# A two-layer decoder trunk on one core: TensorE's order written out for the whole mixer, query weights in the gated blocks' ring, norm factors of the queries in the exponentials' scale

## The chip, the cores and the metric

The kernel runs on one core of a Trainium2 chip. The core has TensorE (PE, matmuls, with weight loads shown apart as PEld), VectorE (DVE), ScalarE (ACT), GpSimd (POOL) and SyncE (SP, which issues most transfers). The metric is the device time of one execution in microseconds (us), lower is better.

## The reference

Two layers on 512 tokens of width 1024, all float32. Each layer is a half-step feed-forward, a mixer, a second half-step feed-forward and a norm. The mixer, which the change touches:

```python
n = rms_norm(h, mix_norm[l])
u_conv, q, k, v, q_mem = jnp.split(n @ w_in[l], splits, axis=-1)   # 768, 384, 128, 128, 256 columns
y_conv = conv_module(u_conv, ...)       # a * sigmoid(gate), causal depthwise conv of 31 taps, layer norm, silu
q = apply_rope(rms_norm(q per head of 64, swa_q_norm[l]), cos, sin)     # 6 heads; k the same, 2 heads
y_swa = sliding_window_attention(q, k, v, swa_sinks[l])                 # blocks of 128, window 128, a sink per head
qm = rms_norm(q_mem per head, mem_q_norm[l])                            # 4 heads
y_mem = memory_attention(qm, mk, mv)                                    # 256 memory tokens
h = h + jnp.concatenate([y_conv, y_swa, y_mem], axis=-1) @ w_out[l]
```

## The kernel before

Activations lie transposed, channels on partitions and 512 tokens along the row. Each float32 product is three products of split operands (`mm3`: hi*hi, lo*hi, hi*lo). A weight tile is loaded to a `raw` tile (3 buffers, SP's queue) and split into `whi` (a rounded copy, ScalarE) and `wlo` (the rest), four buffers each. `wlo` is made in one of two ways: with `V`, VectorE subtracts (L142); with `G`, ScalarE writes -x into it (L147) and GpSimd issues a second transfer of the same weights that adds x (L148). "The gated blocks' ring" is the pool of four `ghi`/`glo` pairs in which the feed-forward keeps its gated activations; the mixer keeps its outputs `y` there.

The engines' instruction streams are put in order by a planner when the program is built: program order is priority, an instruction goes where the planner's own times find room, and a block under `queued()` must follow, on its engine, the last TensorE instruction noted before it (`tail`). On the chip each engine runs its stream in that fixed order.

The mixer's steps follow ORDER (L45). `c0`, `c1`: each conv channel group is two halves (the value and the gate), 24 matmuls each over all tokens; `gate` multiplies by R, the row norm, and by the sigmoid. With c0's first half the sums for the norm are made (rc, a column per token), with its second half R. `q`: for each of four token blocks t, 24 matmuls give 128 tokens by 512 columns (six query heads, two key heads); ScalarE copies them to a half-buffer of the ring `q` (L676) and squares them (L530), VectorE sums the squares (L532, L533), GpSimd raises to the power -1/2 (L189) and makes the rotated part in a second half-buffer of the ring (L682), VectorE multiplies, adds (L686, L688), scales each head by its factor (L537), TensorE transposes the four 128-column pieces (L561) and ScalarE writes qT and kT. `v`: the same for values and memory queries. `a`: attention in ten groups of score blocks (`scored`: scores and minimum, since the columns carry a minus sign; `turned`: exponentials, transposes; `weighted`, `scaled`, `attended`); c20 and c21, the two halves of group c2, are issued inside it. `t0` to `t2`: the taps, 31 passes of VectorE per group (L850, L853), the lowest priority. `s`: layer norm and silu. Then the output product: for eight output blocks first the five attention pieces, then the three conv pieces. PSUM banks: three `mm` and one `cf` taken in turn by `mm()`, two `po`, two `pt`.

Of the kernel before, what the change touches and what calls it, by code (L numbers as in the profile page):

```python
# [10 lines left out]
F32 = mybir.dt.float32  # L11
# [33 lines left out]
ORDER = "c0 c1 q v a t0 t1 t2 s"  # L45
# [14 lines left out]
def trunk(ctx: ExitStack, tc: tile.TileContext, xT, memT, pos, w1a, w3a, w2a, w1b, w3b, w2b,  # L60
# [96 lines left out]
    def weights(src, cols, on):  # L157
        hi, lo = pair()
# [361 lines left out]
    A.activation(maskr, cst[:, 0 : P + 256], AF.Copy)  # L520
# [6 lines left out]
    def head_scale(ps, col, n):  # L527
# [6 lines left out]
        return rsq(v, n)  # L534
# [22 lines left out]
    def to_columns(dst, src, n, tag="pt"):  # L557

        pt = bank([P, n, P], tag)
        for c in range(n):  # L560
            T.transpose(pt[:, c, :], src[:, blk(c)], ident)  # L561
        if dst is not None:
            A.activation(dst, pt[:, 0 : dst.shape[1], :], AF.Copy)
        return pt

    def memory(l):
# [20 lines left out]
        for t in range(2):  # L587
# [6 lines left out]
            A.activation(mT[:, :, blk(t)], to_columns(None, q, 2, "mm"), AF.Copy, scale=-(HD**-0.5))  # L594
# [7 lines left out]
    def mixer(l, x, st, last):  # L602
# [14 lines left out]
        gg = [tmp.tile([P, 2, S], F32, tag="g", name="gg", bufs=2) for _ in range(2)]  # L617
        rings = {"pr": [uu[:, 0], uu[:, 1], tm("pr", "pr", 1)], "q": [x[:, i] for x in gg for i in range(2)],
                 "ptb": [scratch[0][:, blk(i, S)] for i in range(2)], "yn": [scratch[1][:, blk(i, CCH)] for i in range(2)],
                 "cv": [scratch[2][:, blk(i, S)] for i in range(2)]}  # L620
# [39 lines left out]
        conv_halves = []  # L660

        def conv_in(c):
            for i in range(2):
                conv_half(c, i)
            for i in range(2):
                gate(c, i)


        def queries():
            ww = [weights(wqk[l, i], 1024, G) for i in range(4)]  # L670
            for t in range(NT):
                ps = mm()
                for k in range(KD):
                    mm3(ps, at(x, ALL, k, blk(t)), at(ww[k // 2], ALL, blk(k % 2, 512)), k == 0, k == KD - 1)
                q = ring("q")
                A.activation(q, ps, AF.Copy, scale=rc[:, t : t + 1])  # L676
                r = head_scale(ps, rc[:, t : t + 1], 8)
                q2 = ring("q")
                qv, q2v = (z.rearrange("p (h s e) -> p h s e", s=2, e=32) for z in (q, q2))
                for i, (h0, n) in enumerate(((0, NH), (NH, 2))):  # L680
                    for half in range(2):
                        G.tensor_tensor(out=q2v[:, h0 : h0 + n, half, :], in0=qv[:, h0 : h0 + n, 1 - half, :],  # L682
                                        in1=sg[:, t, i, half].unsqueeze(1).to_broadcast([P, n, 32]), op=ALU.mult)
                for i, (h0, n) in enumerate(((0, NH), (NH, 2))):
                    z = heads(q)[:, h0 : h0 + n, :]
                    V.tensor_tensor(out=z, in0=z, in1=cg[:, t, i].rearrange("p s e -> p (s e)").unsqueeze(1).to_broadcast([P, n, HD]),  # L686
# [332 lines left out]
```

## Time and profile before

| | |
|---|---|
| time, median of 3 runs | 1838.69 us (1835.46 to 1841.57) |
| the profiled execution: its time, its span | 1838.87 us, 1836.9 us |
| mean granted TensorE clock | 0.984 |
| busy, share of the span: PE, PEld, DVE, ACT, POOL | 97%, 86%, 71%, 48%, 9% |
| DMA | 243.62 MB, mean 133 GB/s |
| chain that ended last | PE 79%, DVE 11%, issue 7% |

A busy share is a mean over the whole span; the mixers are some 380 to 573 us and 1280 to 1480 us of it. "Idle before" is the time in which an engine stood before an instruction, with what ended the wait.

### The profile page before, as it was taken

The page shows a single profiled execution, that of the slowest core. Times are in us where ns is not written, and L with a number is a line of the kernel's source. Part 1 is how long each engine was busy: PE and PEld are TensorE (multiplying, and loading weights), DVE is VectorE, ACT ScalarE, POOL GpSimd, SP SyncE. Part 2 cuts the span into 40 slices and gives each one's busy share as a digit, 9 for nine tenths or more (in the row PEclk, how much of TensorE's full clock was granted, in tenths as well). Part 3 has the DMA queues.
Part 4 walks back from the last instruction along what each step waited for, and adds up shares of the span by engine and source line. Part 5 has one row for each costly group of instructions (what it writes and reads, how often), then busy time and mean ns, then how long its engine had stood idle before and what let it go on. Part 6 is the DMA issues. An engine that isn't in the chain of part 4 may idle for free.

```text
span 1836.9 us, 28081 instructions
## 1 busy us (share of the span) xinstructions
PE 1773.1 (97%) x10996; PEld 1585.7 (86%) x10996; DVE 1301.3 (71%) x1918; ACT 880.6 (48%) x1350; POOL 173.7 (9%) x179
## 2 busy tenths in 40 slices
PE   8999999997999999999999999999979999999997
PEld 6889999876778989898888898988867879898986
DVE  8967666679757867575678685756788577675755
ACT  4546444444546535353655453535346455353532
POOL 2002000005001000000010010000240010000000
PEclk9999999998999999999999999999979999999998
DMA  7456655262038456565555474643420575474722
GB/s 243 110 166 174 171 135 150 58 155 68 16 91 203 109 145 169 142 165 140 156 132 150 142 185 137 167 115 109 97 71 10 145 161 151 134 181 123 173 77 80
DMA packets 91284, 243.62 MB, mean 133 GB/s; under 512 B 9360, under 2 KB 11664, under 8 KB 91152
## 3 DMA queue, kind: packets, MB, share of 16 engines
q1 hardware_dynamic: 77040, 190.45, 33.9%
q0 software_dynamic: 14112, 51.39, 15.6%
q8 instruction: 86, 1.41, 0.3%
q14 instruction: 46, 0.38, 0.1%
HBM read 239.70 MB, written 2.10 MB: 132 GB/s over the span
## 4 chain that ended last, share of the span: by engine, by line
PE 79%; DVE 11%; issue 7%; ACT 1%; DMA 1%; POOL 0%; SPq 0%; DVEq 0%; POOLq 0%; ACTq 0%
PE mm L173 11%; PE mm L172 11%; PE mm L174 11%; PE po L172 9%; PE po L173 9%; PE po L174 9%; PE pt L173 6%; PE pt L172 6%; PE pt L174 6%; DVE there L853 4%; DVE wlo L142 1%; DVE xlo L152 1%; DVE st L240 1%; DVE nmw L745 1%; PE cf L172 1%
## 5 line engine op out<-in xcount | busy, mean ns | idle before, releaser
L141 ACT ACTIVATE whi<-raw 128x1024 fp32r<-128x1024 f32 (+4 forms) x384 | 353.6, 924 | 510.1 <-PE mm L173 240.8
L142 DVE TENSOR_TENSOR wlo<-raw,whi 128x1024 fp32r<-128x1024 f32 (+4 forms) x384 | 404.7, 1056 | 134.7 <-ACT whi L141 133.2
L173 PE MATMUL mm<-glo,whi 128*128 128x512 f32 x752 | 293.8, 391 | 0.0
L174 PE MATMUL mm<-ghi,wlo 128*128 128x512 f32 x752 | 292.9, 389 | 0.0
L172 PE MATMUL mm<-ghi,whi 128*128 128x512 f32 x752 | 291.0, 390 | 0.0
L174 PE MATMUL po<-mh,wlo 128*128 128x256 f32 x864 | 244.6, 283 | 1.4 <-DVE wlo L142 1.4
L172 PE MATMUL pt<-xhi,whi 128*128 128x256 f32 x864 | 243.2, 283 | 2.1 <-ACT xhi L141 2.0
L173 PE MATMUL pt<-xlo,whi 128*128 128x256 f32 x864 | 243.8, 283 | 1.6 <-DVE xlo L142 1.6
L172 PE MATMUL po<-mh,whi 128*128 128x256 f32 x864 | 244.8, 283 | 0.4 <-ACT part L380 0.4
L173 PE MATMUL po<-ml,whi 128*128 128x256 f32 x864 | 244.6, 283 | 0.0
L174 PE MATMUL pt<-xhi,wlo 128*128 128x256 f32 x864 | 243.7, 283 | 0.0
L458 DVE SCALAR_TENSOR_TENSOR h<-mm,h 128x512 f32<-128x512 f32 x128 | 87.7, 688 | 138.5 <-PE mm L174 138.4
L172 PEld LDWEIGHTS pt<-xhi,whi 128*128 128x128 f32 x864 | 165.1, 192 | 3.6 <-ACT xhi L141 2.4
L173 PEld LDWEIGHTS pt<-xlo,whi 128*128 128x128 f32 x864 | 165.7, 192 | 2.6 <-DVE xlo L142 1.8
L174 PEld LDWEIGHTS po<-mh,wlo 128*128 128x128 f32 x864 | 165.8, 192 | 1.6 <-DVE wlo L142 1.6
L172 PEld LDWEIGHTS po<-mh,whi 128*128 128x128 f32 x864 | 165.8, 192 | 1.5 <-ACT part L380 0.8
L174 PEld LDWEIGHTS mm<-ghi,wlo 128*128 128x128 f32 x752 | 141.2, 188 | 29.7 <-issue 0.5
L172 PEld LDWEIGHTS mm<-ghi,whi 128*128 128x128 f32 x752 | 141.1, 188 | 29.3 <-DVE h L458 1.2
L173 PEld LDWEIGHTS po<-ml,whi 128*128 128x128 f32 x864 | 165.8, 192 | 0.6
L173 PEld LDWEIGHTS mm<-glo,whi 128*128 128x128 f32 x752 | 141.3, 188 | 28.3 <-issue 0.5
L174 PEld LDWEIGHTS pt<-xhi,wlo 128*128 128x128 f32 x864 | 165.5, 192 | 0.0
L853 DVE SCALAR_TENSOR_TENSOR there<-ypad,par,there 128x512 f32<-128x512 f32 x180 | 133.4, 755 | 1.0
(283 smaller groups left out, 3243.4 us busy)
## 6 DMA issues: line engine op xcount, KB each, us to landing
raw<-in_w2a SPq DMA_DIRECT2D x48, 384.0 KB, 3.7
raw<-in_w2b SPq DMA_DIRECT2D x48, 384.0 KB, 3.6
raw<-in_w1b SPq DMA_DIRECT2D x26, 512.0 KB, 3.7
raw<-in_w3b SPq DMA_DIRECT2D x26, 512.0 KB, 3.7
raw<-in_w1a SPq DMA_DIRECT2D x25, 512.0 KB, 3.7
raw<-in_w3a SPq DMA_DIRECT2D x25, 512.0 KB, 4.2
wsum<-in_w1a SPq DMA_DIRECT2D x18, 512.0 KB, 4.5
wsum<-in_w3a SPq DMA_DIRECT2D x18, 512.0 KB, 4.5
```

The source lines that it names most:

```text
L141: A.activation(hi, x, AF.Copy)
L142: on.tensor_tensor(out=lo, in0=x, in1=hi.bitcast(F32), op=ALU.subtract)
L152: V.scalar_tensor_tensor(out=lo, in0=x, scalar=col, in1=hi.bitcast(F32), op0=ALU.mult, op1=ALU.subtract)
L172: T.matmul(ps, a[0], b[0], start=first, stop=False, **more)
L173: T.matmul(ps, a[0], b[1], start=False, stop=False, **more)
L174: tail[0] = T.matmul(ps, a[1], b[0], start=False, stop=last, **more)
L240: V.tensor_tensor(out=self.sums[0], in0=self.sums[0], in1=sq, op=ALU.add)
L458: V.scalar_tensor_tensor(out=h[:, d, :], in0=ps, scalar=0.5, in1=h[:, d, :], op0=ALU.mult, op1=ALU.add)
L745: V.tensor_reduce(out=each(nmw, i), in_=pp[i], axis=AX.X, op=ALU.min)
L853: V.scalar_tensor_tensor(out=cv[:, c, :], in0=ypad[:, c, j : j + S], scalar=conv_w[:, c, j : j + 1], in1=cv[:, c, :], op0=ALU.mult, op1=AL ...
```

## The change

`ORDER` names every conv half, query block, value block and transposition on its own, and all of them are put under `queued()`, so TensorE's order is that of the list. The transpositions (`Q0` to `Q3`, `V0` to `V3`) are steps of their own, each some steps behind its block. c20 stands in the list; c21 follows the first scores. The query weights, and those of c20 and c21, take pairs of the gated ring (`spare()`); the four pairs for `y` are taken later, inside attention and in reverse. Every query block has its own buffer, with q2 in the two halves of `uu`. The query heads and the memory queries are transposed without their norm factors (rq, rm): scores take a maximum, one small VectorE step multiplies it by minus the factor, and the exponential gets the factor as its scale; only the two key heads are scaled before the transposition. The minus sign leaves kT and mT and goes into the mask. c1, c2 and the first four output products' weights are split with `G`; the sums for the sinks (esw) go from VectorE to GpSimd.

```diff
-ORDER = "c0 c1 q v a t0 t1 t2 s"
+ORDER = "c00 c01 q0 c10 q1 Q0 c11 q2 Q1 v0 q3 Q2 v1 v2 Q3 V0 v3 V1 c20 V2 V3 a t0 t1 t2 s"
...
-    def weights(src, cols, on):
-        hi, lo = pair()
+    def weights(src, cols, on, own=None):
+        hi, lo = own or pair()
...
-    A.activation(maskr, cst[:, 0 : P + 256], AF.Copy)
+    A.activation(maskr[:, 0:P], cst[:, 0:P], AF.Copy)
+    A.activation(maskr[:, P : P + 256], cst[:, P : P + 256], AF.Copy, scale=-1.0)
...
-    def head_scale(ps, col, n):
+    def head_scale(ps, col, n, out=None):
...
-        return rsq(v, n)
+        if out is None:
+            return rsq(v, n)
+        G.tensor_tensor(out=out, in0=v, in1=nhalf[:, 0:n], op=ALU.pow)
...
-        gg = [tmp.tile([P, 2, S], F32, tag="g", name="gg", bufs=2) for _ in range(2)]
-        rings = {"pr": [uu[:, 0], uu[:, 1], tm("pr", "pr", 1)], "q": [x[:, i] for x in gg for i in range(2)],
...
+        query = [tmp.tile([P, 2, S], F32, tag="g", name="query", bufs=2) for _ in range(2)]
...
+        def spare():
+
+            return tuple(z.rearrange("p i s -> p (i s)") for z in gated_pair())
...
-            with queued() if c == 2 or 2 * c + i < 3 else nullcontext():
-                project(ps, weights(wconv[l, c, i], 1024, V), x)
+            with queued():
+                project(ps, weights(wconv[l, c, i], 1024, G if c else V, spare() if c == 2 else None), x)
...
-            conv_halves.append(ps)
-            if c == 2:
-                gate(c, i)
+            halves.append((c, i, ps))
+            while halves and R is not None:
+                gate(*halves.pop(0))
...
+        def queries(t):
+            if not t:
+                ww["q"] = [weights(wqk[l, i], 1024, G, spare()) for i in range(4)]
+            ps = mm()
+            with queued():
                 for k in range(KD):
...
+            q, q2 = query[t // 2][:, t % 2], uu[:, t % 2]
+            A.activation(q, ps, AF.Copy, scale=rc[:, t : t + 1])
+            head_scale(ps, rc[:, t : t + 1], 8, rq[:, t, :])
...
+            V.tensor_tensor(out=q, in0=q, in1=q2, op=ALU.add)
+            per_head(q[:, CCH:], rq[:, t, NH:], 2)
+
+        def query_columns(t):
+            with queued():
+                pt = to_columns(qT[:, :, blk(t)], query[t // 2][:, t % 2], 4)
+            A.activation(kT[:, blk(t)], pt[:, CC, :], AF.Copy, scale=HD**-0.5)
...
+        def values(t):
+            if not t:
+                ww["v"] = [weights(wvm[l, i], 768, V) for i in range(4)]
...
-                per_head(q, head_scale(ps[:, 0:256], rc[:, t : t + 1], NM), NM)
-                to_columns(qmT[:, :, blk(t)], q, 2, "po")
+            q = scratch[0][:, blk(t, 256)]
+            A.activation(q, ps[:, 0:256], AF.Copy, scale=rc[:, t : t + 1])
+            head_scale(ps[:, 0:256], rc[:, t : t + 1], NM, rm[:, t, :])
+
+        def value_columns(t):
+            with queued():
+                to_columns(qmT[:, :, blk(t)], scratch[0][:, blk(t, 256)], 2, "po")
...
-                    V.tensor_reduce(out=nmr[:, b, i], in_=pp[i], axis=AX.X, op=ALU.min)
+                    V.tensor_reduce(out=nmr[:, b, i], in_=pp[i], axis=AX.X, op=ALU.max)
+                V.scalar_tensor_tensor(out=nmr[:, b], in0=nmr[:, b], scalar=-1.0, in1=by_half(rm[:, b, :]), op0=ALU.mult, op1=ALU.mult)
...
-                V.tensor_reduce(out=each(nmw, i), in_=pp[i], axis=AX.X, op=ALU.min)
+                V.tensor_reduce(out=each(nmw, i), in_=pp[i], axis=AX.X, op=ALU.max)
+            V.scalar_tensor_tensor(out=at_(nmw), in0=at_(nmw), scalar=-1.0, in1=rr, op0=ALU.mult, op1=ALU.mult)
...
-            V.tensor_tensor(out=at_(esw), in0=at_(nmw), in1=per(sinks), op=ALU.add)
+            G.tensor_tensor(out=at_(esw), in0=at_(nmw), in1=per(sinks), op=ALU.add)
...
-                A.activation(pr[:, i, 0:W], scores[i], AF.Exp, bias=nm[:, b, i, c : c + 1], scale=-1.0)
+                n = 2 * c + i
+                A.activation(pr[:, i, 0:W], scores[i], AF.Exp, bias=nm[:, b, i, c : c + 1], scale=rr[:, b, n : n + 1])
...
             s = scored(GROUPS[0][0], GROUPS[0][1:])
+            conv_half(2, 1)
+            yy.extend([gated_pair() for _ in range(KD // 2)][::-1])
+            y.extend(at(p, ALL, i, ALL) for p in yy for i in range(2))
...
-                if n < 2:
-                    conv_half(2, n)
                 nxt_s = None
-                if 2 <= n + 1 < len(GROUPS):
+                if n + 1 < len(GROUPS):
...
-            w = weights(wout[l, d, :, CCH:], 640, V)
+            w = weights(wout[l, d, :, CCH:], 640, G if d < 4 else V)
```

## Rows read from the trace of the kernel before

**Rows 1.** The page's first part: busy time of each engine, its share of the span, and the count of its instructions.

```profile
PE 1773.1 (97%) x10996; PEld 1585.7 (86%) x10996; DVE 1301.3 (71%) x1918; ACT 880.6 (48%) x1350; POOL 173.7 (9%) x179
```

**Rows 2.** Busy time by stage, the two mixer stretches (us): length, busy time of PE, PEld, DVE, ACT and POOL with the count of instructions, mean granted clock of PE, DMA share, GB/s.

```profile
380.00:573.00 193.00, 174.76 (x937) 143.51 (x936) 148.77 (x273) 95.60 (x180) 39.21 (x37) 0.95 0.34 87
1280.00:1480.00 200.00, 181.61 (x959) 148.43 (x957) 152.59 (x273) 99.28 (x186) 39.00 (x37) 0.94 0.35 91
```

**Rows 3.** The same view in narrower slices, around the second half of the queries and values in layer 0 and layer 1.

```profile
440.00:460.00 20.00, 6.54 (x28) 3.92 (x26) 20.00 (x42) 8.61 (x21) 7.28 (x5) 0.65 0.21 66
448.00:464.00 16.00, 8.43 (x27) 5.54 (x28) 15.86 (x32) 6.16 (x14) 4.81 (x4) 0.50 0.13 41
1346.00:1366.00 20.00, 7.63 (x35) 5.04 (x34) 20.00 (x39) 10.36 (x23) 7.29 (x5) 0.61 0.21 67
```

**Rows 4.** TensorE's waits, first in 376 to 575 us, then in 1281 to 1473 us: what waited for whom, us in total, times, longest.

```profile
PE pt L561 <- DVE gg L537: 8.1, 1, 8.1
PE po L561 <- DVE gg L537: 4.6, 2, 3.0
PE mm L173 <- DVE xlo L152: 1.4, 4, 0.6
PE po L561 <- DVE hv L533: 0.9, 1, 0.9
...
PE pt L561 <- DVE gg L537: 6.3, 1, 6.3
```

**Rows 5.** TensorE's timeline: start, us, line, operation. First eight score matmuls in the hole and eight later; then, in layer 1, two transposes of L561 with the wait ahead of them (in brackets), the first matmul of c20 and what follows its last, and the same of c21.

```profile
454.77 2.08 PE L730 MATMUL mm<-mT,there 64*128 64x256 f32 x8 [0.47 <-ACT there L563]
487.30 1.14 PE L730 MATMUL mm<-here 64*128 64x256 f32 x8
1358.79 0.66 PE L561 MATMUL po<-cst,gg 128*128 128x128 f32 x2 [3.03 <-DVE gg L537]
1365.83 0.66 PE L561 MATMUL po<-cst,gg 128*128 128x128 f32 x2 [1.60 <-DVE gg L537]
1366.14 0.78 PE L172 MATMUL po<-xhi,whi 128*128 128x512 f32 x1
1373.98 1.03 PE L761 MATMUL pt<-cst,uu 128*128 128x128 f32 x8
1377.36 0.50 PE L172 MATMUL po<-xhi,whi 128*128 128x512 f32 x1
1382.93 0.51 PE L724 MATMUL mm<-maskr 128*128 128x384 f32 x2
```

**Rows 6.** Timelines of ScalarE, VectorE and GpSimd in layer 0: the fourth query block from its copy to its scaling.

```profile
434.82 0.70 ACT L676 ACTIVATE gg<-cf,rc 128x512 f32<-128x512 f32 x1
442.02 0.16 DVE L533 TENSOR_SCALAR hv<-hs 128x8 f32<-128x8 f32 x1
442.33 2.48 POOL L189 TENSOR_TENSOR rsq<-hv,nhalf 128x8 f32<-128x8 f32 x1 [3.16 <-DVE hv L533]
448.69 0.68 DVE L537 TENSOR_TENSOR gg<-gg,rsq 128x512 f32<-128x512 f32 x1
```

**Rows 7.** The query weights: SP's raw loads in layer 0, GpSimd's issue of the last accumulating transfer, and, for all accumulating transfers of L148, the time from issue to landing.

```profile
374.72 10.18 SPq L99 DMA_DIRECT2D raw<-in_wqk  x4
403.20 0.86 POOL L148 DMA_DIRECT2D wlo<-in_wqk  x1 [4.62 <-ACT wlo L147]
DMA to landing us min/median/max: 5.6/7.8/10.4
```

**Rows 8.** GpSimd's power -1/2, groups by line and shape: count, busy us and mean ns of one, idle before.

```profile
L189 POOL TENSOR_TENSOR rsq<-hv,nhalf 128x8 f32<-128x8 f32 x8 | 19.7, 2458 | 18.5 <-DVE hv L533 18.5
L189 POOL TENSOR_TENSOR rsq<-hv,nhalf 128x4 f32<-128x4 f32 x12 | 19.6, 1636 | 77.2 <-DVE hv L533 77.2
L189 POOL TENSOR_TENSOR rsq<-ms,nhalf 128x4 f32<-128x4 f32 x9 | 9.6, 1068 | 154.9 <-DVE ms L203 153.7 <-DVE pf L481 1.2
```

**Rows 9.** VectorE's share of the work: busy times from the first gate to the output product in layer 0 and layer 1; the taps (L853), ns min/median/max; and groups by shape of layer 0 in 391.5 to 519.9 us.

```profile
391.50:519.20 127.70, 110.84 (x642) 91.74 (x641) 114.20 (x216) 60.49 (x129) 31.68 (x29) 0.92 0.21 52
1297.00:1424.00 127.00, 111.72 (x648) 92.68 (x647) 112.67 (x210) 61.85 (x129) 31.64 (x29) 0.92 0.20 52
L853 DVE SCALAR_TENSOR_TENSOR there<-ypad,par,there x180: 720/742/1086, 394.9 to 1421.4; 128x512 f32<-128x512 f32 x180
...
L142 DVE TENSOR_TENSOR wlo<-raw,whi 128x640 fp32r<-128x640 f32 x4 | 3.3, 814 | 0.0
L537 DVE TENSOR_TENSOR gg<-gg,rsq 128x512 f32<-128x512 f32 x4 | 3.1, 777 | 0.2 <-POOL rsq L189 0.2
L142 DVE TENSOR_TENSOR wlo<-raw,whi 128x1024 fp32r<-128x1024 f32 x2 | 2.4, 1214 | 0.0
L537 DVE TENSOR_TENSOR gg<-gg,rsq 128x256 f32<-128x256 f32 x4 | 1.6, 411 | 0.0
```

**Rows 10.** Timelines of VectorE and TensorE at the mixer's end in layer 0: the last tap, the start of the output product, the low part of the last conv output, the first matmul that takes conv outputs.

```profile
516.53 0.75 DVE L853 SCALAR_TENSOR_TENSOR there<-ypad,par,there 128x512 f32<-128x512 f32 x1
518.92 0.95 PE L172 MATMUL mm<-ghi,whi 128*128 128x512 f32 x3
546.35 0.69 DVE L142 TENSOR_TENSOR glo<-aux,ghi 128x512 fp32r<-128x512 f32 x1 [1.08 <-ACT ghi L141]
549.90 0.39 PE L172 MATMUL mm<-ghi,whi 128*128 128x512 f32 x1
```

More of the change, by code (lines that the diff above doesn't have):

```diff
@@ L560, in to_columns @@
         for c in range(n):
-            T.transpose(pt[:, c, :], src[:, blk(c)], ident)
+            tail[0] = T.transpose(pt[:, c, :], src[:, blk(c)], ident)
         if dst is not None:
@@ L626, in ring @@
             return r[-1]
-        yy = [gated_pair() for _ in range(KD // 2)]
-        y = [at(p, ALL, i, ALL) for p in yy for i in range(2)]
         R, rc = None, const.tile([P, NT], F32, tag="rc", name="rc")
+        ww = {}
+        def spare():
+            return tuple(z.rearrange("p i s -> p (i s)") for z in gated_pair())
         def conv_half(c, i):
@@ L644, in conv_half, with gate @@
                         R = kept(spread(rc), "R")
-            conv_halves.append(ps)
-            if c == 2:
-                gate(c, i)
-        def gate(c, i):
+            halves.append((c, i, ps))
+            while halves and R is not None:
+                gate(*halves.pop(0))
+        halves = []
+        def gate(c, i, ps):
             u = ypad[:, c, PAD:]
-            ps = conv_halves.pop(0)
             if not i:
@@ L658, in gate @@
             V.tensor_tensor(out=u, in0=u, in1=s, op=ALU.mult)
[L660 to L672, printed above, removed]
-                for k in range(KD):
[L674 to L686, printed above, removed]
-                                    op=ALU.mult)
-                V.tensor_tensor(out=q, in0=q, in1=q2, op=ALU.add)
-                per_head(q, r, 8)
-                pt = to_columns(qT[:, :, blk(t)], q, 4)
-                A.activation(kT[:, blk(t)], pt[:, CC, :], AF.Copy, scale=-(HD**-0.5))
@@ L694, in values @@
-        def values():
-            ww = [weights(wvm[l, i], 768, V) for i in range(4)]
-            for t in range(NT):
-                ps = mm()
-                for k in range(KD):
-                    mm3(ps[:, 0:CCH], at(x, ALL, k, blk(t)), at(ww[k // 2], ALL, blk(k % 2, CCH)), k == 0, k == KD - 1)
-                A.activation(vn[:, t, :, 0:HD], heads(ps[:, 256:CCH]), AF.Copy, scale=rc[:, t : t + 1])
-                q = ring("q")[:, 0:256]
-                A.activation(q, ps[:, 0:256], AF.Copy, scale=rc[:, t : t + 1])
-                per_head(q, head_scale(ps[:, 0:256], rc[:, t : t + 1], NM), NM)
-                to_columns(qmT[:, :, blk(t)], q, 2, "po")
+        rq = const.tile([P, NT, 8], F32, tag="rq", name="rq")
@@ L710, in mixer @@
+        def value_columns(t):
+            with queued():
+                to_columns(qmT[:, :, blk(t)], scratch[0][:, blk(t, 256)], 2, "po")
+        yy, y = [], []
         nmw, esw = (const.tile([P, NT, 2, CC], F32, tag=t, name=t) for t in ("nmw", "esw"))
         nmr = const.tile([P, NT, 2, 2], F32, tag="nmr", name="nmr")
-        sinks, nsinks = (z.rearrange("p (c i) -> p i c", i=2) for z in (sink, nsink[:, l, :]))
+        by_half = lambda z: z.rearrange("p (c i) -> p i c", i=2)
+        sinks, nsinks = by_half(sink), by_half(nsink[:, l, :])
@@ L875, in mixer @@
         for step in ORDER.split():
-            f = {"c": conv_in, "q": queries, "v": values, "a": attention, "t": taps, "s": swish}[step[0]]
+            f = {"c": conv_half, "q": queries, "Q": query_columns, "v": values, "V": value_columns, "a": attention, "t": taps,
+                 "s": swish}[step[0]]
             f(*map(int, step[1:]))
```

26 lines of the change are left out of this document (20 added, 6 removed).

## The prediction

> **What bounds the kernel now.** I read the totals first: TensorE is busy for 97% of the span [rows 1], so at most some 60 us of plain idleness can be won anywhere, and every other engine has room on average. The second view is the busy time by stage: the two mixer stretches hold 174.8 us of TensorE in 193 us and 181.6 us in 200 us, at a mean granted clock of 0.95 and 0.94 [rows 2]. About 18 us is lost in each of two stretches that make a fifth of the span. Cutting them into 20 us slices shows one hole: in 440 to 460 us TensorE works 6.5 us of 20 while VectorE works all 20, and the granted clock is 0.65 there, with 0.50, the lower of its two levels (1.2 GHz for 2.4), all through 448 to 464 us; layer 1 has the same hole at 1346 us [rows 3]. The third view, TensorE's own waits, names it: the transposes of L561, queries and memory queries, wait 8.1 + 4.6 + 0.9 us in layer 0 [rows 4] and 6.3 + 3.0 + 1.6 us in layer 1 [rows 4, 5] for VectorE's L537 and L533, the norm factors.
>
> The timelines show why the factors are late. ScalarE takes the fourth query block out of PSUM only at 434.8 us, behind the columns of an earlier one, because the ring "q" has four half-buffers and each block takes two (q and q2). After that its chain is long: its mean square is ready at 442.0, GpSimd's power starts at 442.3 and takes 2.5 us, and VectorE's L537 starts at 448.7, 13.9 us after the copy [rows 6]. TensorE has nothing else in that time: c20 (L638, group c2) stands behind attention's first scores, and these behind the transposes. The clock halves in the hole, which costs again after it: eight score matmuls take 2.08 us against 1.14 us later, and c20 in layer 1 takes 1373.98 - 1366.14 = 7.84 us where c21 takes 1382.93 - 1377.36 = 5.57 us [rows 5].
>
> **What the change wins.** TensorE's instructions are the same in number and size; what can go is the waiting and the half clock.
> 1. Layer 0's waits on L561, and the L730 that follows: 8.1 + 4.6 + 0.9 + 0.5 = 14.1 us. Layer 1: 6.3 + 3.0 + 1.6, and layer 0's 0.9 and 0.5 again: 12.3 us [rows 4, 5].
> 2. Half clock: c20 7.84 - 5.57 = 2.3 us, the scores 2.08 - 1.14 = 0.9 us, the 12 transposes of the hole by the same ratio some 1.8 us (an estimate from those two ratios) [rows 5]. 5.0 us in each layer, 10.0 us in all.
> Together 14.1 + 12.3 + 10.0 = 36.4 us.
>
> Is the cover there? In the new order Q0 stands behind c10 and q1, Q1 behind c11 and q2, Q2 behind v0 and q3, Q3 behind v1 and v2. A conv half or a query block is 24 matmuls, 5.5 us like c21 [rows 5]; a value block has 384 of 512 columns, about 4.2 us. So the covers are 11, 11, 9.7 and 8.4 us. The chain of 13.9 us shrinks: each query block now has its own buffer; the six query heads leave their factors to the exponentials. What remains is the two key heads' product on 128 of the 512 columns that L537 takes now, but the power is still awaited for it. Without VectorE's queue I count copy and square 1.3, reduction and small step 0.9, power 2.5, sum and product 1.0: 5.7 us, and with a tap of 0.74 us ahead of each VectorE step about 9 us. So Q0 to Q2 are covered and Q3 is about 0.5 us short; nothing to 5.5 us (the old chain of 13.9 against 8.4) are the bounds, and I take 0.8 us a layer. The memory queries need only a ScalarE copy now, and V0 to V3 stand far behind it.
>
> 3. VectorE is relieved. The wlo halves of c20 and c21 (2.4 us), those of the first four output products (four of the 3.3 us group), the query product on 384 of its 512 columns (4 x some 0.45) and the value product (1.6 us) leave it: 9.1 us [rows 9]. Ten small steps for the factors come, six small sums for the sinks go to GpSimd; at 0.16 us each, as the small step of [rows 6], that is 0.6 us more. Net 8.5 us off 114.2 us [rows 9]. TensorE gets none of it directly: it is what lets the taps end with a shorter attention. The wlo halves of c10 and c11 leave the entrance too, where TensorE waits 1.4 us for xlo behind a full VectorE [rows 4]. Between nothing and 1.4 us a layer I take 1.0.
>
> **What it costs.** For each layer:
> - Query weights. q0 is now second after c0, some 11 us earlier than before (c1 stood ahead of it), and needs all four pairs within its 5.5 us. Before, the fourth pair's accumulating transfer was issued at 403.2, and a transfer takes 5.6 to 10.4 us, 7.8 in the middle; the raw loads were issued from 374.7 to 384.9 behind c10 and c11 [rows 7]. In the gated ring two pairs are free a quarter early and two at the end of the feed-forward; the loads move ahead of c1's, about 5 us. The last raw load at some 378, landing and copies to 384, 7.8 us more: 392, against q0's second half at 394. Bounds: 0 and, at the slowest transfer with a queue on top, 4 us. I take 0.8.
> - V3. c20, V1 to V3 share the two "po" banks: V3 takes c20's bank and cannot start until VectorE's L653 has emptied it. That is one pass over 128x512, by its nearest row (the taps, 0.72 to 1.09) plus one tap ahead, less V2's 0.35: 0.4 to 1.5 us. I take 1.0. Behind V3 all of attention is queued.
> - Attention: one small step between maximum and exponential in ten groups, 0.16 us each or, with a tap ahead, 0.9. The next group's scores cover most: 0 to 5 us, I take 0.7.
> - Accumulating loads for c10 to c21 and four output products: eight more GpSimd issues, ScalarE's copies. ScalarE is busy half the time in the hole [rows 3]; the transfers have 10 us and more ahead of c2 and 40 us ahead of the output products. Nothing, unless something ahead of them on GpSimd's queue waits: then the query factors queue with them.
> - The tail. The last tap begins at 516.5, attention ends and the output product starts at 518.9, the last conv output is ready at 547.0 and is wanted at 549.9 [rows 10]: slack 2.9 us. If attention ends about 18 us earlier, VectorE has 127.7 - 18 = 110 us for 114.2 - 8.5 = 105.7 us [rows 9]. That just fits; the taps are late relative to attention by 1 to 5 us. 0 to 3 us, I take 1.0.
> Sum of costs: 0.8 + 0.8 + 1.0 + 0.7 + 1.0 = 4.3 us a layer, 8.6 us.
>
> **The sum.** 36.4 + 2.0 - 8.6 = 29.8 us off the profiled execution's 1838.87 us: 1809 us. The median of the runs is 1838.69, the same for this purpose. With every cost at nothing and the whole 2.8 us of the entrance it is 1838.9 - 39.2 = 1800; with the costs doubled 1818. That is the likeliest case's own range.
>
> **Rule and rows on GpSimd.** The power that fills rq takes 1.64 us for 128x4 in the heads' form and 1.07 us in the form of L203, where VectorE has little to do [rows 8]; a tap, with two operands in SBUF, takes 0.720 to 1.086 us [rows 9]. So the two engines slow each other, by at most 0.37 us a tap. The Trainium skill (SBUF — State Buffer, "Who interferes with whom") says more: a VectorE instruction with two SBUF inputs and a GpSimd instruction that reads SBUF exclude each other, and the second waits for the whole of the first. By the row, twelve sums moved to GpSimd cost VectorE at most 12 x 0.37 = 4.4 us in two layers; by the rule, whole operations. The difference is a rival.
>
> **The rivals.**
> - VectorE becomes the bound. It needs 105.7 us in layer 0; at today's share of 114.2 in 127.7 us (89%) that takes 118 us, so only 9.6 us a layer are won: 1838.9 - 19 = 1820, from 1817 to 1826. For it: VectorE is full through the hole [rows 3]. Against it: its idle time lies after the hole, in c20 and c21, where TensorE gave it nothing.
> - No change: each of the twelve sums on GpSimd holds a tap and what queues behind it for as long as the 128x8 power, 2.46 us: 12 x 2.46 = 29.5 us, the whole gain, 1838. For it: the power's own length [rows 8]; against it: no tap of 180 exceeds 1.086 us [rows 9].
> - Slower: the query weights come as late as now. If the last transfer lands as before at 403.2 + 7.8 = 411 while q0 wants it at 394, TensorE stands 17 us, the clock halves and costs another 5 us, and everything behind, in fixed order, is late by it: 22 - 15 (the net gain of a layer) = 7 us a layer lost, 1853. It decides from a delay of about 10 us on. Against it: today's issues are spaced by slots that c0 and c1 hold, and the gated ring is free by then.
>
> **How the numbers follow.** A measurement of this kernel tells about 0.3% (5.5 us) from no change; its three runs spread from 1835.5 to 1841.6. Likeliest 0.66; VectorE bound 0.21; no change 0.05; slower 0.05; a gain beyond the likeliest's bounds, if the entrance and the attention's own small waits go too, 0.03. The range 1798 to 1827 takes the first two cases with their bounds and leaves out the rest. Faster 0.89, same 0.05, slower 0.06.
>
> **What would show it.** Right: in the slices between the first gate and attention TensorE is full and the clock 1.0; L561 no longer waits for L537 by microseconds; c20 takes 5.6 us, as c21 does; the output product starts 15 to 18 us earlier after the entrance than now. The weak places would show as TensorE waits: at q0 for a DMA or ScalarE (weights), at V3 for L653, at Q3 for L537, in the output product for L871's splits (the tail). Wrong: a wait of over 5 us at any of these with the clock falling after it, or taps that end more than 8 us behind attention.

## The result and the profile after

The changed kernel takes 1820.41 us, median of 5 runs (1818.45 to 1827.55), for 1838.69 before; the ratio of all runs is 0.9914, 95% interval 0.9885 to 0.9944, which stands for 15.8 us (10 to 21). The profiled execution is the quickest of the five; it spans 1816.7 us, 20.2 us less than that of the kernel before, at a mean granted clock of 0.996. The page's totals, to be read beside [rows 1], and the two mixer stretches [rows 2]:

```profile
PE 1763.6 (97%) x10996; PEld 1578.3 (87%) x10996; DVE 1281.8 (71%) x1902; ACT 899.6 (50%) x1367; POOL 192.3 (11%) x207
380.00:565.00 185.00, 172.35 (x942) 141.80 (x940) 140.11 (x264) 103.76 (x188) 46.19 (x49) 0.99 0.44 109
1270.00:1462.00 192.00, 178.47 (x973) 146.19 (x973) 142.89 (x266) 109.98 (x195) 49.81 (x53) 1.00 0.46 115
```

The same 10996 matmuls keep TensorE busy 9.5 us less; the account below puts 10.7 us of half clock given back into the two mixers. The hole of [rows 3] is shallow now; what is left of it lies at 430 to 440 us:

```profile
440.00:460.00 20.00, 18.21 (x99) 15.68 (x98) 18.86 (x37) 9.80 (x22) 9.78 (x8) 1.00 0.55 127
430.00:440.00 10.00, 7.23 (x33) 7.03 (x34) 10.00 (x20) 2.53 (x6) 7.36 (x8) 0.83 0.72 138
```

TensorE's waits in 365 to 565 us, beside [rows 4]:

```profile
PE pt L566 <- DVE query L542: 2.6, 2, 1.3
PE cf L176 <- DMA wlo<-in_wconv: 1.6, 1, 1.6
PE pt L566 <- DVE query L690: 1.5, 1, 1.5
PE pt L778 <- ACT uu L772: 1.4, 2, 0.8
PE pt L778 <- ACT aux L780: 1.4, 3, 0.6
PE po L789 <- ACT aux L780: 1.0, 2, 0.8
...
PE po L566 <- ACT there L568: 0.5, 1, 0.5
...
PE mm L175 <- DMA glo<-in_wqk: 0.2, 1, 0.2
```

L566 are the transposes (L561 before), L690 is the sum that ends a query block's rotation, L542 the key heads' product, L568 ScalarE's copy of the transposed columns, L176 with `wlo<-in_wconv` c10's wait for its accumulating transfer, L772 the exponentials, L780 the copy of their transposes. Blocks count from 0: Q2 are the third block's transposes, Q3 the fourth's. No single wait is over 1.6 us, but layer 0's mixer has eighteen of them.

**One account for all kernels.** Take a mixer from its first conv matmul to the first matmul of the output product, subtract TensorE's waits of over 0.15 us, with the one at that last matmul, and its busy time lost at half clock ((1 - granted clock) x busy, summed over 2 us slices): what remains is 119.1 to 121.1 us in every profile of this study, 14 kernels and both layers. So a mixer is some 120 us plus waits plus half clock, and the table says where each kernel's time is. Waits in us: at the entrance / at the query and value transposes / in c20, c21 and attention; then + half clock. The waits are those of one profiled execution each, not of the median.

| kernel | median us, ratio (95%) | layer 0 | layer 1 |
|---|---|---|---|
| before | 1838.69 | 143.2: 1.1 / 13.7 / 2.6 + 5.5 | 142.8: 1.2 / 11.9 / 2.6 + 6.9 |
| changed | 1820.41, 0.9914 (0.9885 to 0.9944) | 134.4: 2.6 / 4.6 / 4.8 + 1.7 | 133.4: 3.2 / 4.5 / 4.7 + 0 |
| e1 | 1818.70, 0.9908 (0.9893 to 0.9922) | 134.2: 3.7 / 2.3 / 4.8 + 3.4 | 130.7: 2.9 / 1.2 / 4.8 + 1.7 |
| e2 | 1820.50, 0.9920 (0.9904 to 0.9935) | 137.1: 3.1 / 3.8 / 4.0 + 6.3 | 130.5: 3.2 / 2.0 / 4.5 + 0 |
| e3 | 1829.45, 0.9963 (0.9951 to 0.9975) | 139.6: 2.6 / 3.6 / 9.1 + 3.3 | 135.3: 3.0 / 2.1 / 7.4 + 1.7 |
| e4 | 1814.18, one run | 132.4: 1.9 / 4.7 / 2.1 + 4.1 | 129.7: 3.1 / 2.6 / 2.1 + 1.6 |
| e5 | 1828.64, 0.9951 (0.9936 to 0.9966) | 140.9: 3.0 / 1.9 / 8.3 + 8.1 | 134.6: 3.1 / 0.5 / 6.7 + 3.3 |
| e6 | 1824.44, 0.9937 (0.9917 to 0.9957) | 138.1: 2.6 / 1.3 / 6.2 + 8.5 | 134.1: 3.0 / 1.3 / 6.0 + 3.3 |
| e7 | 1824.72, 0.9939 (0.9920 to 0.9957) | 141.7: 3.0 / 6.1 / 4.0 + 9.6 | 133.8: 3.0 / 4.1 / 3.7 + 3.4 |
| e8 | 1834.98, 0.9995 (0.9986 to 1.0005) | 142.3: 1.4 / 12.6 / 2.7 + 4.6 | 140.7: 1.6 / 11.5 / 2.6 + 4.5 |
| e9 | 1814.91, 0.9895 (0.9878 to 0.9911) | 134.9: 1.3 / 3.8 / 4.0 + 6.3 | 128.7: 1.5 / 2.2 / 4.7 + 0 |
| e10 | 1827.85, 0.9961 (0.9946 to 0.9975) | 139.2: 1.3 / 6.0 / 5.2 + 6.8 | 136.4: 1.4 / 3.8 / 5.7 + 4.7 |
| e11 | 1825.11, 0.9934 (0.9916 to 0.9952) | 136.2: 3.0 / 3.2 / 4.7 + 4.9 | 134.5: 3.0 / 2.9 / 5.8 + 2.5 |
| e12 | 1812.17, 0.9866 (0.9847 to 0.9884) | 128.7: 0.9 / 0.5 / 6.3 + 1.7 | 129.4: 1.2 / 0.7 / 6.7 + 0 |

Ratios are to runs of the kernel before on the same chip; medians come from several chips. Change against before: 8.8 and 9.4 us a mixer, so 18.2 of the 20.2 us between the two profiles.

### The profile page after: what moved, and what is told of

Same layout as the page of the kernel before. It is cut to its first block, busy times and chain, and to the rows that moved or that the text cites. A ratio compares the mean times of both kernels' runs of the same rounds, so it can differ in the third digit from the quotient of the medians.

```text
span 1816.7 us, 28098 instructions
## 1 busy us (share of the span) xinstructions
PE 1763.6 (97%) x10996; PEld 1578.3 (87%) x10996; DVE 1281.8 (71%) x1902; ACT 899.6 (50%) x1367; POOL 192.3 (11%) x207
## 4 chain that ended last, share of the span: by engine, by line
PE 75%; DVE 12%; issue 6%; DMA 4%; ACT 2%; SPq 0%; POOLq 0%; DVEq 0%; POOL 0%; ACTq 0%
PE mm L174 10%; PE mm L175 10%; PE mm L176 10%; PE po L174 8%; PE po L176 8%; PE po L175 8%; PE pt L175 6%; PE pt L174 6%; PE pt L176 6%; DVE there L869 5%; DVE wlo L144 1%; DMA raw<-in_wvm 1%; DMA raw<-in_wconv 1%; DVE nmw L760 1%; PE cf L174 1%
## 5 line engine op out<-in xcount | busy, mean ns | idle before, releaser
L143 ACT ACTIVATE whi<-raw 128x1024 fp32r<-128x1024 f32 (+3 forms) x368 | 339.2, 925 | 481.8 <-PE mm L175 233.4
L144 DVE TENSOR_TENSOR wlo<-raw,whi 128x1024 fp32r<-128x1024 f32 (+3 forms) x368 | 388.9, 1058 | 156.2 <-ACT whi L143 154.9
L176 PE MATMUL mm<-ghi,wlo 128*128 128x512 f32 x752 | 292.6, 389 | 0.0
L176 PE MATMUL po<-mh,wlo 128*128 128x256 f32 x864 | 244.6, 283 | 1.4 <-DVE wlo L144 1.4
L176 PE MATMUL pt<-xhi,wlo 128*128 128x256 f32 x864 | 243.7, 283 | 0.0
L176 PEld LDWEIGHTS po<-mh,wlo 128*128 128x128 f32 x864 | 165.8, 192 | 1.6 <-DVE wlo L144 1.6
L176 PEld LDWEIGHTS mm<-ghi,wlo 128*128 128x128 f32 x752 | 141.3, 188 | 29.8 <-issue 0.5
L176 PEld LDWEIGHTS pt<-xhi,wlo 128*128 128x128 f32 x864 | 165.5, 192 | 0.0
L869 DVE SCALAR_TENSOR_TENSOR there<-ypad,par,there 128x512 f32<-128x512 f32 x180 | 135.7, 762 | 1.4
```

The costliest lines, as they stand in the source:

```text
L143: A.activation(hi, x, AF.Copy)
L144: on.tensor_tensor(out=lo, in0=x, in1=hi.bitcast(F32), op=ALU.subtract)
L176: tail[0] = T.matmul(ps, a[1], b[0], start=False, stop=last, **more)
L869: V.scalar_tensor_tensor(out=cv[:, c, :], in0=ypad[:, c, j : j + S], scalar=conv_w[:, c, j : j + 1], in1=cv[:, c, :], op0=ALU.mult, op1=AL ...
```

## The experiments

### What made the factors late: e8

Only the buffers, in the kernel before:

```diff
...
-                q = ring("q")
+                q, q2 = gg[t // 2][:, t % 2], uu[:, t % 2]
...
-                q = ring("q")[:, 0:256]
+                q = scratch[0][:, blk(t, 256)]
```

> The kernel before, with nothing changed but the buffers of query and value blocks: each query block has its own half-buffer, its rotated copy one of two others, each memory query a quarter of a third. Theory A (the ring of four half-buffers made the hole, as the prediction's second paragraph has it: ScalarE could take the fourth block only at 434.8 us): the two transposes' waits of 8.1 and 4.6 us in layer 0 shrink to under 5 us together and the clock stays up: 1820 to 1828. Rival (the chain itself on VectorE and GpSimd, or the planner's order with its taps, makes the factors late): waits of 9 us and more stay, 1834 to 1840.

ScalarE now takes the fourth block at 423.0 us, 11.8 us earlier than in [rows 6]; VectorE's head sums (L532) of it start at 439.39, for 438.63 before, and its product at 446.90, 1.8 us earlier than before:

```profile
423.00 0.69 ACT L676 ACTIVATE gg<-cf,rc 128x512 f32<-128x512 f32 x1 [0.51 <-PE cf L174]
439.39 0.68 DVE L532 TENSOR_REDUCE hs<-hsq 128x8 f32<-128x512 f32 x1
446.90 0.68 DVE L537 TENSOR_TENSOR gg<-gg,rsq 128x512 f32<-128x512 f32 x1
424.00:448.00 24.00, 18.20 (x107) 17.64 (x108) 24.00 (x43) 9.82 (x23) 11.16 (x8) 0.92 0.38 115
```

The square is done at 424.3 and its sum waits 15 us on a VectorE that works all 24 us of the last row. The ring did not make the hole: with the operand 11.8 us earlier the sum starts no earlier. What VectorE's stream has ahead of it did: in those 15 us six taps (4.4 us), four splits of weights (4.5 us), the rotation tables and steps of the other blocks. This is read from the rows; no run moves the sum forward in the kernel before. The time is unchanged.

### Why Q2 and Q3 wait after the change: e5, e4, e3, e11

In the changed kernel ScalarE's square of the third block is done at 421.9 and of the fourth at 431.3; VectorE, from 423.5:

```profile
423.53 0.81 DVE L869 SCALAR_TENSOR_TENSOR there<-ypad,par,there 128x512 f32<-128x512 f32 x1
...
424.73 2.07 DVE L869 SCALAR_TENSOR_TENSOR there<-ypad,par,there 128x512 f32<-128x512 f32 x3
426.71 0.68 DVE L535 TENSOR_REDUCE hs<-hsq 128x8 f32<-128x512 f32 x1
...
433.89 3.07 DVE L869 SCALAR_TENSOR_TENSOR there<-ypad,par,there 128x512 f32<-128x512 f32 x4
436.88 0.67 DVE L535 TENSOR_REDUCE hs<-hsq 128x8 f32<-128x512 f32 x1
```

L869 are taps: both sums (L535) come some 5 us after their squares, with taps written into the stream ahead of them. e5 writes them behind:

```diff
+PINS = {(0, 19): ("sum", 2), (1, 1): ("sum", 2), (0, 22): ("hs", 3), (1, 2): ("hs", 3)}
...
             for j in range(1, TAPS):
+                ahead = PINS.get((c, j))
+                with tc.issue_after(pins[ahead].ins) if ahead else nullcontext():
                     V.scalar_tensor_tensor(...)
```

> The changed kernel, but on VectorE the norm sums and the rotation of the last two query blocks stand ahead of taps: tap 19 of the first conv group and tap 1 of the second may only be issued behind the third block's sum (L690), tap 22 and tap 2 only behind the fourth block's head sums (L535). The number of instructions is that of the changed kernel. Theory A (the query transposes wait because VectorE's order has taps written ahead of their head sums: the third block's sums start 4.8 us and the fourth's 5.6 us after ScalarE's square is done): the waits of Q2 and Q3, 4.1 us in layer 0 and 4.0 us in layer 1 in the changed kernel, fall under 1 us in each layer, the half clock behind Q2 in layer 0 goes too, the output product starts 3 to 5 us earlier after the entrance: 1810 to 1814 us. Theory B (VectorE is full and is the bound): the waits go from the queries to attention, the time stays at 1818 to 1822. Theory C (the chain waits for GpSimd's power and products): the waits stay within 1 us of what they were, 1818 to 1822.

The mechanism is A: layer 1 has no query wait left, layer 0 keeps 1.2 us at Q3. The time is not: 1828.64, no better than the change (the intervals overlap). The taps that were held back now stand in attention, 40 of them behind c21 in each layer for 32 in the change. They stand ahead of its maxima (L761), whose exponentials TensorE awaits (2.94 us at 484.9), and half clock follows:

```profile
478.57 2.22 DVE L872 SCALAR_TENSOR_TENSOR there<-ypad,par,there 128x512 f32<-128x512 f32 x2
480.70 0.68 DVE L761 TENSOR_REDUCE nmw<-mm 128x2 f32<-128x512 f32 x1
PE pt L779 <- ACT uu L773: 5.0, 3, 2.9
484.00:494.00 10.00, 9.10 (x42) 7.78 (x42) 9.24 (x20) 6.08 (x16) 0.84 (x2) 0.53 0.00 0
```

e4 leaves out 15 of the 31 taps of every group, 45 passes a layer:

```diff
-            for j in range(1, TAPS):
+            for j in range(1, 16):
```

> The changed kernel with 15 of the 31 taps left out in every group, so the conv is not the reference's; 45 passes of 0.74 us, 30 us a layer, leave VectorE. If VectorE's load makes the waits (A and B): no wait at L566 above 0.5 us, attention's waits (4.8 us a layer) fall by half, clock 1.0; 1798 to 1806 us. If the waits are the length of the chain itself, ScalarE, GpSimd's power and TensorE (C): the waits of L566 stay within 1 us of 4.1 a layer; 1815 us or more. The 1.6 us of c10 and the late R stay in both.

VectorE is busy for 26 us less in each mixer (85.1 us for 111.5 in layer 0); the mixers win 2.0 and 3.7 us, in a single run. Attention's waits are halved; those of the queries stay in layer 0 and nearly halve in layer 1, for taps are written ahead of the fourth block's sums here too, and GpSimd lengthens one of them and the small step behind the sum:

```profile
435.78 2.19 DVE L869 SCALAR_TENSOR_TENSOR there<-ypad,par,there 128x512 f32<-128x512 f32 x1
435.67 2.46 POOL L684 TENSOR_TENSOR uu<-query,sg 128x192 f32<-128x192 f32 x4
441.00 1.25 DVE L536 TENSOR_SCALAR hv<-hs 128x8 f32<-128x8 f32 x1
440.29 1.93 POOL L875 TENSOR_TENSOR aux<-there 128x512 f32<-128x512 f32 x1 [2.17 <-DVE there L869]
```

The tap's median is 0.74 us and the small step takes 0.16 elsewhere, so some 2.5 of the 4.3 us for which layer 0's Q3 waits here are GpSimd's (an estimate from these rows). VectorE's total is not the bound; what stands ahead of a sum is.

e3 takes q3 ahead of v0 in ORDER and so puts more between q3 and Q3 (first added line); e11 puts Q3 behind v3 (second):

```diff
-ORDER = "c00 c01 q0 c10 q1 Q0 c11 q2 Q1 v0 q3 Q2 v1 v2 Q3 V0 v3 V1 c20 V2 V3 a t0 t1 t2 s"
+ORDER = "c00 c01 q0 c10 q1 Q0 c11 q2 Q1 q3 v0 v1 Q2 v2 Q3 v3 V0 V1 c20 V2 V3 a t0 t1 t2 s"
+ORDER = "c00 c01 q0 c10 q1 Q0 c11 q2 Q1 v0 q3 Q2 v1 v2 V0 v3 Q3 V1 c20 V2 V3 a t0 t1 t2 s"
```

> The changed kernel with the order alone altered: q3 ahead of v0, and Q2 behind v1, Q3 behind v2, which gives Q2 13.9 us and Q3 about 13 us of cover instead of 9.7 and 8.4. Theory C (cover too short): the waits of L566 (4.1 us a layer) and the half clock after them (some 1.6 us) go and nothing comes in their place: 1808 to 1811 us. Theories A and B (VectorE is late as a whole): the waits of L566 go, but half of them or more come back in attention, where VectorE's maxima stand behind taps, or in the output product: 1814 to 1819 us.

> The changed kernel with one step of TensorE's order moved: the fourth query block's transposes (Q3) stand behind the fourth value block and V0 (V0 v3 Q3 for Q3 V0 v3), so that they have 4 us more of matmuls ahead of them. Nothing else is changed. Theory A (Q3 waits because its cover is too short for VectorE's chain): its wait of 1.3 us in layer 0 and 1.2 us in layer 1 goes, and nothing takes its place: 2.5 us less, 1816 to 1819, up to 2 us more where a half clock goes with it. Theory B (the wait moves on to the value transposes or to attention, whose steps stand in the same VectorE order): within 1 us of the changed kernel in the gaps, 1819 to 1822.

e3: the query waits shrink by 1.0 and 2.4 us, and c20 and c21 wait for their banks instead, 3.3 us in each layer (L568, L660): slower than the change, the intervals apart. e11: Q3's wait is gone in both layers as A says, attention's waits are the same in layer 0 and 1.1 us longer in layer 1, but half clock costs 3.2 and 2.5 us more. 1825.11 us lies above both theories' times, and the interval overlaps the change's: nothing won.

### The entrance: e1, e2, e9

ScalarE and VectorE before c0's gate in the changed kernel:

```profile
393.80 0.84 ACT L143 ACTIVATE whi<-raw 128x768 fp32r<-128x768 f32 x1 [2.42 <-DMA raw<-in_wvm]
397.01 0.84 ACT L143 ACTIVATE whi<-raw 128x768 fp32r<-128x768 f32 x1 [2.37 <-DMA raw<-in_wvm]
397.75 0.58 ACT L217 ACTIVATE R<-pt 128x512 f32<-128x512 f32 x1
394.67 0.96 DVE L144 TENSOR_TENSOR wlo<-raw,whi 128x768 fp32r<-128x768 f32 x1 [9.01 <-ACT whi L143]
375.70:400.00 24.30, 21.67 (x100) 16.82 (x98) 7.90 (x13) 15.01 (x18) 5.44 (x6) 1.00 1.04 266
```

R's matmuls start at 388.73, but R's copy (L217) stands behind two copies of value weights that wait for transfers; VectorE idles 9 us for them and the first tap (L866) starts at 401.47, for 394.28 before. The DMA engines are full in this stretch (share 1.04, 266 GB/s; before 0.65 and 162).

e1 splits c1's weights on VectorE again (first pair of lines); e2 holds ScalarE's copies of the value weights behind c0's sigmoid, `copied[0]` (second); e9 does both and holds c1's splits behind rc's copy, `copied[1]` (third):

```diff
-                project(ps, weights(wconv[l, c, i], 1024, G if c else V, spare() if c == 2 else None), x)
+                project(ps, weights(wconv[l, c, i], 1024, G if c == 2 else V, spare() if c == 2 else None), x)
...
+                with tc.issue_after(copied[0].ins):
+                    ww["v"] = [weights(wvm[l, i], 768, V) for i in range(4)]
...
+            with tc.issue_after(copied[1].ins) if c == 1 else nullcontext():
+                w = weights(wconv[l, c, i], 1024, G if c == 2 else V, spare() if c == 2 else None)
```

> The changed kernel with one part undone: c10 and c11 are split by VectorE's subtraction again, so two accumulating transfers of 512 KB leave each mixer's entrance. Theory A (transfers crowd the entrance: 7.5 MB in 374 to 404 us, the value weights land late, their copies stand ahead of R's copy on ScalarE, the first tap starts at 401.5 us instead of 394.3 and VectorE stays late): the value weights land 4 to 6 us earlier, the first tap starts at 396 to 398, c10's 1.6 us wait is gone, the waits of L566 fall from 4.1 us a layer to 2 or less; 1809 to 1813 us. Theory B (VectorE simply has too much to do between queries and taps, whenever it starts): the 2.4 us that come back to VectorE fall into its idle time, the waits of L566 stay; only c10's wait goes, 1817 us. Theory C (the cover ahead of Q2 and Q3 is too short for the chain): as B.

> The changed kernel with one thing moved: on ScalarE the copies of the value weights are issued behind the sigmoid of c0's gate instead of ahead of R's copy; the transfers stay as they are. Theory A: R's copy at 390.5 us instead of 397.8, c0's gate done by 394, the first full tap at 398 to 399 (two low halves of the value weights still stand ahead of it), VectorE 2 to 3 us less late; the waits of L566 fall by 1 to 3 us a layer; 1814 to 1818 us. Theories B and C: VectorE's start does not matter, 1819 to 1821 us.

> The changed kernel with three edits at the entrance: the weights of the second conv group are split on VectorE again and not by GpSimd's accumulating transfers, these two splits may only be issued behind the copy of the columns' norm factors (L648 in the changed kernel), and ScalarE's copies of the value weights only behind the first gate's sigmoid. The arithmetic is unchanged. Theory A (each engine serves in order, and at the entrance ScalarE's and VectorE's steps for c0's gate stand behind copies that wait for weight transfers; what is late there comes back at Q2 and Q3): the waits for c10's accumulated weights (1.6 us) and for the norm factors (3.0 and 2.2 us in the run with the second group on VectorE alone) are both gone, the first tap starts 5 us earlier, Q2 waits under 0.5 us; gaps of 8 to 9.5 us a layer for 12.0 and 12.5, and with the clock up 1808 to 1814 us. Theory B (VectorE's total is the bound): 1816 to 1822. Theory C (the clock decides): the gaps fall as in A, but half clock follows one of the waits that stay and takes 3 to 8 us of it back: 1813 to 1818.

e1: c10's wait for its transfer goes; a new one of 3.0 and 2.2 us comes, since rc's copy (L648) stands on VectorE behind c1's splits, which wait for ScalarE and it for the raw loads. e2: R's copy comes at 392.08; Q2's wait goes, Q3's stays. Neither time can be told from the change's, and both medians lie above their theory A. e9 frees the entrance of both waits: R's copy at 390.49, first tap at 395.96, entrance waits 1.3 and 1.5 us:

```profile
390.49 0.58 ACT L217 ACTIVATE R<-pt 128x512 f32<-128x512 f32 x1
PE pt L566 <- DVE query L694: 2.0, 1, 2.0
PE pt L566 <- DVE query L542: 1.3, 1, 1.3
```

Theory A for the gaps, C for the time: Q3's wait in layer 0 stays (the last two rows, 3.4 us) and the mixer loses 6.3 us at half clock; layer 1 keeps 1.7 us of Q3's wait, loses nothing at half clock and takes 128.7 us. The interval overlaps the change's.

### The parts undone: e6, e10, e7

e6 takes `queued()` from queries and values; e10 does so and restores the old sequence:

```diff
-ORDER = "c00 c01 q0 c10 q1 Q0 c11 q2 Q1 v0 q3 Q2 v1 v2 Q3 V0 v3 V1 c20 V2 V3 a t0 t1 t2 s"
+ORDER = "c00 c01 c10 c11 q0 Q0 q1 Q1 q2 Q2 q3 Q3 v0 V0 v1 V1 v2 V2 v3 V3 c20 a t0 t1 t2 s"
```

> The changed kernel with the first part undone for queries and values: their matmuls and transposes are no longer fixed behind the one before, the planner places them; conv halves and attention stay fixed, weights and norm factors stay as changed. Theory A (the fixed order is what wins): the hole at the query transposes opens again with a wait of 3 us or more, 1826 to 1838. Rival (own buffers and shorter chains win, the order is nothing): 1816 to 1823, with the waits of the changed kernel.

> The changed kernel with the first part undone altogether for queries and values: their TensorE work is placed by the planner, as in the run with the order left free, and the steps are handed to it in the order of the kernel before: both conv groups, then each query block with its transposes, then each value block with its transposes, then the third conv group and attention. Own buffers, query weights in the gated ring and norm factors stay as changed. Theory A (the new sequence, with queries and values between the conv halves, is what closes the hole): the hole is back at the query and value transposes, 9 us of waits or more in each mixer and half clock after it, 1828 to 1838. Theory B (the shorter chain, with the six query heads' factors left to the exponentials, closes it): waits under 5 us at the transposes, 1818 to 1825.

e6: the intervals overlap, so fixing the order as such is not shown to win; the query waits are even shorter. e10 is slower than the change, the intervals just apart, by 7 us in the medians: the sequence counts. But the hole is not back (6.0 and 3.8 us at the transposes for 13.7 and 11.9), so something else closes most of it too. Which part does is not shown: e10 keeps the own buffers, the query weights' place, c20 ahead of attention, the splits with `G` and the norm factors, and only the own buffers were tried alone (e8: not they).

e7 undoes the norm factors' part:

```diff
-            per_head(q[:, CCH:], rq[:, t, NH:], 2)
+            per_head(q, rq[:, t, :], 8)
...
+            per_head(q, rm[:, t, :], NM)
...
-            V.scalar_tensor_tensor(out=at_(nmw), in0=at_(nmw), scalar=-1.0, in1=rr, op0=ALU.mult, op1=ALU.mult)
...
-                A.activation(pr[:, i, 0:W], scores[i], AF.Exp, bias=nm[:, b, i, c : c + 1], scale=rr[:, b, n : n + 1])
+                A.activation(pr[:, i, 0:W], scores[i], AF.Exp, bias=nm[:, b, i, c : c + 1], scale=-1.0)
```

> The changed kernel with the third part undone: the norm factors are again multiplied into all eight heads of a query block and into the memory queries before the transposes, the exponentials' scale is -1, the ten small steps at the maxima are gone. VectorE gets four products of 128x384 (0.55 us) and four of 128x256 (0.41) and loses ten steps of 0.15: 2.3 us more a layer. Theory A (only the chain ahead of Q2, Q3 and the value transposes counts): the query waits grow by 0.3 to 0.5 us each and V's transposes wait for power and product: 2 to 6 us more in all, 1822 to 1827. Theory B (VectorE's load is the bound, us for us): 4.6 us more, 1824 to 1826, with the waits in attention. Rival (the small steps at the maxima are what made attention's waits grow from 2.5 to 4.8 us): attention's waits fall back under 3.5 us a layer and the time does not rise: 1816 to 1821.

```profile
PE pt L565 <- DVE query L541: 4.1, 2, 3.6
PE po L787 <- ACT aux L778: 2.0, 1, 2.0
PE po L565 <- DVE aux L541: 2.0, 1, 2.0
```

Part of both holds, of A and of the rival: attention's waits fall by 0.8 and 1.0 us, less than half of what they had grown by, and one of 2.0 us at the memory queries is back in layer 0. The query waits change little, half clock grows by 7.9 and 3.4 us. The medians say 4 us for this part; the intervals overlap. The hole is not back here either: in the new sequence it stays closed without this part. No run undoes the query weights' place, the splits with `G` of c20, c21 and the output products, or the sums on GpSimd.

### Together: e12

e9's edits, e11's order, and layer 1's tables behind the fourth block's last product, `copied[2]`:

```diff
     def tables(l):
+        with tc.issue_after(copied[2].ins) if l else nullcontext():
+            tables_of(l)
```

> The three edits at the entrance (second conv group's weights split on VectorE behind the norm factors' copy, ScalarE's copies of the value weights behind the first sigmoid), Q3 behind the fourth value block, and layer 1's rotation tables (L556, L558 of the changed kernel, 2.1 us on VectorE in layer 0's mixer) held back until the fourth query block's last product. Theory A (all that is left at the queries is cover and order): Q2's and Q3's waits go in both layers (3.4 and 1.7 us in the run with the entrance alone), gaps of 5.5 to 7 us a layer, and the half clock behind Q3 in layer 0 (3.4 us) goes with its wait: 1805 to 1811 us. Theory B (VectorE's total is the bound, so the waits go to attention): 1812 to 1816. Theory C (the half clock strikes at another wait): 1809 to 1815 with gaps as in A and a loss of 3 us or more somewhere in attention.

```profile
1274.00:1450.00 176.00, 167.39 (x925) 138.50 (x925) 139.68 (x256) 98.37 (x180) 44.74 (x47) 1.00 0.41 103
PE pt L787 <- ACT uu L781: 2.8, 2, 2.0
PE po L798 <- ACT aux L789: 1.3, 1, 1.3
```

Faster than both kernels: 1812.17 us, its interval just below the change's. The transposes wait 0.5 and 0.7 us. Attention's waits grow to 6.3 and 6.7 us and the time lies in B's range, so part of B holds. Of this, about 1.1 us in layer 1 is GpSimd's: a small step (L756, at 1355.02) takes 1.23 us beside one of its sums, for 0.16 elsewhere.

## Why the prediction was right, and where it was not

1809 us were forecast and 1820 measured: inside the range, but 2 us beyond the likeliest case's own bounds (1818 with the costs doubled). The range holds it because it was drawn to take in the rival's 1817 to 1826 as well; for the likeliest case's sum that is luck. 14.9 us a layer were to be won and 9.1 were, in the mixers. Of the signs, c20 takes 5.6 us and c21 5.7, and the clock in the mixers is 0.99 and 1.00; but the transposes still wait 1.2 to 1.5 us three times in each layer, and the output product starts 8.8 and 9.4 us earlier after the entrance, not 15 to 18.

- **Waits at the transposes** (14.1 and 12.3 us, of which Q3 should keep 0.8): right in place, wrong in size, 4.6 and 4.5 us are left. The step that failed is "The chain of 13.9 us shrinks" to "about 9 us" by "a tap of 0.74 us ahead of each VectorE step". From copy to key product the fourth block takes 430.04 to 444.83, 14.8 us; the third 12.3. Four taps stand ahead of one sum. So Q2, called covered, waits 2.8 us, more than Q3 with 1.3; and Q3's wait is that short only because Q2's waits and the half clock behind them stretch its cover from 8.4 to 13.8 us (430.04 to 443.85). Its premise on the ring of half-buffers fell with e8.
- **Half clock** (5.0 us a layer): 3.8 and 6.9 given back.
- **Entrance** (1.0 us won): nothing. The 1.4 us were read from a row over 376 to 575 us, and only 0.9 of them lie at the entrance; there VectorE is busy for 14.7 of 24.3 us, not full, and 0.8 us stay, for xhi and xlo. c10 waits 1.6 us for its accumulating transfer, which was costed at nothing. Copies that wait for transfers also delayed the gate (e2, e9).
- **Query weights** 0.8: 0.2 and 0.7. **V3** 1.0: 0.5, for ScalarE's L568, not VectorE's gate. **Tail** 1.0: nothing, the last taps end at 502.0 and the output product starts at 509.83.
- **Attention** 0.7: 2.7 and 2.6 (4.8 and 4.7 less 2.6, of which 0.5 was L730's wait). e4 and e7 point to the cause, small steps with taps ahead: each takes part of it away, neither all.

Of the forecast, 5.8 us a layer are missing. By these terms they are some 3.3 us at the queries, 1.6 at c10, 1.0 of the entrance and 2.0 in attention, less 1.5 that V3 and the tail did not cost and 0.7 by which half clock and the query weights did better: 5.7 us.

**The rivals.** "VectorE becomes the bound" named the time, 1820, but not the mechanism: e4 takes away a quarter of its busy time in the mixers for 5.7 us, and e12 wins 8 us with all of it. Its premise, a share of 89%, did not hold either: in the change VectorE is busy for 104.6 of the 111.1 us from the first gate (398.7) to the output product, 94%. GpSimd's sums for the sinks did not hold the taps: they take 0.20 to 0.65 us there, not 2.46, and a tap's median is 743 ns for 742, its longest 1091 for 1086. By the Trainium skill's rule (SBUF — State Buffer, "Who interferes with whom") a tap would wait for GpSimd's whole instruction; in the change no tap is lengthened by more than 0.35 us over the median, beside products of 0.6 to 1.4 us. In seven of the twelve other runs, though, one or two taps take 1.96 to 2.30 us beside a row of GpSimd's products of about 0.6 to 1.2 us (e3 at 433.49, e4 at 435.78, e9 at 431.20), 1.2 to 1.6 us over the median. So the rule isn't refuted, and the 0.37 us a tap that was the prediction's bound from [rows 9] is too low. Query weights were not late.

What stays open: why half clock falls behind one wait and not behind its like, and so what e6 and e7 cost beyond it; and which of the parts that e10 keeps closes the hole.

## What to carry to other kernels

An engine that is "full" with low-priority work is a matter of order before it is one of load: look at how many fillers stand between an operand's arrival and the short step that a busy engine waits for, and hold the fillers back there, but count where they go. A copy that waits for a transfer blocks everything behind it on its engine; issue it behind the steps that need no transfer. Read waits and lost clock as separate terms: 1.2 us of wait were followed by some 7 us at half clock in e9 and by none in the change.

## What the runs showed of the hardware

The granted clock does not follow from the waits alone. In the changed kernel and in e9 the same two waits in attention, 0.80 and 0.40 us, end at 497.06 and 499.19 and at 495.70 and 497.83; TensorE's granted clock in the stretch after them, e9 first:

```profile
498.00:506.00 8.00, 8.00 (x43) 6.78 (x42) 4.62 (x12) 4.31 (x11) 1.46 (x2) 0.57 0.00 1
498.00:506.00 8.00, 6.95 (x57) 5.75 (x55) 5.80 (x16) 6.02 (x16) 1.47 (x2) 1.00 0.00 0
```

Both had been at half clock (0.5, 1.2 GHz) once before, behind a query wait: e9 from 440 to 447 us, the changed kernel from 433 to 437. Of the changed kernel's five runs the one of 1818.45 us has a mean clock of 0.996 and that of 1827.55 us 0.990; 0.006 x 1820 = 11 us is the most that this difference can cost, so the clock alone can make that spread of 9 us.

A VectorE step can be lengthened beside GpSimd by more than one GpSimd instruction takes: the tap at 435.78 in e4 takes 2.19 us for 0.74, 1.45 us more, beside four products of 0.6 to 1.1 us. In all runs every tap of over 1.1 us overlaps GpSimd's work.
